# Seventeen feed-forward pairs by seven half-size products each, and the down projection as a stage behind them

## The chip, the cores and the metric

The kernel runs on one core of a Trainium2 chip. The core has a matrix engine (TensorE, PE in the profile), a vector engine (VectorE, DVE), an activation engine (ScalarE, ACT), a general engine (GpSimd, POOL) and queues that start DMA transfers (SyncE, SP). Each engine runs its own instructions in order and waits for others by semaphores. SBUF is the memory that the engines compute in, PSUM the small memory into which PE writes products. The metric is the device time of one launch in microseconds (us), as the median of several runs.

## What is computed

One step of a decoder layer for 1024 prompt tokens and 8 x 4 sample tokens, 1056 in all, all in float32: a combined projection, two attention-like branches, an output product with a norm, and then the part that the change touches, the convolutional feed-forward:

```python
def _conv_ffn(h, cbuf, w_up, b_up, conv_w, conv_b, w_down, b_down):
    L = h.shape[1]
    u = h @ w_up + b_up                                   # 1024 -> 5632
    ux = jnp.concatenate([cbuf.astype(u.dtype), u], axis=1)
    y = conv_b + ux[:, 0:L] * conv_w[0]
    for j in range(1, CONV_W):                            # CONV_W = 3
        y = y + ux[:, j:j + L] * conv_w[j]
    a, g = y[..., :D_FF], y[..., D_FF:]                   # D_FF = 2816
    out = (jax.nn.gelu(a) * g) @ w_down + b_down          # 2816 -> 1024
    return out, ux[:, L:]
...
    h2 = _ln(x) * (1.0 + sc2) + sh2
    f, cbuf_new = _conv_ffn(h2, cbuf, w_up, b_up, conv_w, conv_b, w_down, b_down)
    x = _ln(ALPHA * x + g2 * f, ln2_g, ln2_b)
```

## The kernel before

Activations lie transposed: a tile holds 128 features on the partitions and the 1056 tokens along the free axis. Full precision comes from operands in two parts. An operand x is cast to a reduced type that PE takes at speed (`hi`, by ACT), and `lo = x - hi` is made by DVE. `group()` (L440) then makes every product as three: hi·hi, hi·lo and lo·hi, added up in one PSUM bank.

The up projection has 44 blocks of 128 features, in 22 pairs (block j is the gelu half, block 22 + j its factor). A block takes 8 chunks of the input `h2` by 3 parts by 3 token tiles (384, 384 and 288 tokens, `TT`), so 72 matmuls. `Stream` (L387) loads each block's weights in one DMA (128 x 1024), `prep` casts the high part on ACT (L424) and subtracts the low part on DVE (L428). `up_evac` (L1504) moves a finished token tile out of PSUM on ACT with the bias (L1511). `post` (L1537) then runs the causal convolution of three taps on DVE (L1519, L1524 twice, three small ones for the sample tokens at L1531 to L1533; POOL only copies a few columns), the gelu on ACT (L1546), the product of the two halves on DVE (L1550) and the split into `acts2` (L336, L337).

After every third pair a down group (`down_group`, L1659) multiplies the three finished blocks with `w_down` and adds to the accumulators `facc` (L1680). Six such groups lie between the up blocks. `pre` (L1605) gathers their sums by tokens, and the last group of four blocks ends the program, a token block at a time, with the last norm (`product`, `add`, `stats`, `gains`).

The order of work is written by hand. PE's products are emitted in their order, and `pulse` hands out steps of the generators in `sides` at a rate per us of products (`RATES`), so a step of a convolution stands between two products of the program text. SBUF is cut into 43 slots (`NSLOT`), given out in the order in which they came back.

## Time and profile before

| | |
|---|---|
| median of 3 runs | 1984.14 us (1982.23 to 1985.65) |
| span of the profiled execution | 1981.8 us |
| PE busy | 1942.6 us, 98% |
| DVE busy | 997.7 us, 50% |
| ACT busy | 723.3 us, 36% |
| POOL busy | 308.9 us, 16% |
| first up block to last | about 1161 to 1915 us, with six down groups between |
| last matmul to the end | about 16 us |

The span is counted from the first to the last instruction that the profiler saw; the runs are timed from outside it. A "busy" matmul overlaps the one before it, so PE's pace is read from the distance between two starts, not from one's duration.

### The profile page before, as it was taken

The page shows a single profiled execution, that of the slowest core. Times are in us where ns is not written, and L with a number is a line of the kernel's source. Part 1 is how long each engine was busy: PE and PEld are TensorE (multiplying, and loading weights), DVE is VectorE, ACT ScalarE, POOL GpSimd, SP SyncE. Part 2 cuts the span into 40 slices and gives each one's busy share as a digit, 9 for nine tenths or more (in the row PEclk, how much of TensorE's full clock was granted, in tenths as well). Part 3 has the DMA queues.
Part 4 walks back from the last instruction along what each step waited for, and adds up shares of the span by engine and source line. Part 5 has one row for each costly group of instructions (what it writes and reads, how often), then busy time and mean ns, then how long its engine had stood idle before and what let it go on. Part 6 is the DMA issues. An engine that isn't in the chain of part 4 may idle for free. (4 is left out here: it accounts for less than half of the span.)

```text
span 1981.8 us, 31279 instructions
## 1 busy us (share of the span) xinstructions
PE 1942.6 (98%) x12597; PEld 1858.1 (94%) x12597; DVE 997.7 (50%) x2166; ACT 723.3 (36%) x1522; POOL 308.9 (16%) x592
## 2 busy tenths in 40 slices
PE   6999999999999999999999999999999999999996
PEld 4899999999998989999999999999999999999995
DVE  4454444444544535241454455564554554645579
ACT  4534334343546445331312454353131312222331
POOL 2013223231123131200000333100000000000007
PEclk9999999999999999999999999999999999999998
DMA  9151424324220322497524142111212020211533
GB/s 289 47 140 25 140 35 119 84 70 100 69 76 23 112 72 60 136 345 244 159 65 128 54 129 67 36 38 48 60 35 62 28 69 27 63 34 49 194 130 130
DMA packets 214362, 187.86 MB, mean 95 GB/s; under 512 B 8849, under 2 KB 197953, under 8 KB 214185
## 3 DMA queue, kind: packets, MB, share of 16 engines
q1 hardware_dynamic: 213437, 185.26, 31.1%
q8 instruction: 98, 1.61, 0.3%
q10 hardware_dynamic: 780, 0.61, 0.1%
q14 instruction: 47, 0.39, 0.1%
HBM read 150.06 MB, written 37.81 MB: 95 GB/s over the span
## 5 line engine op out<-in xcount | busy, mean ns | idle before, releaser
L450 PE MATMUL L<-hhi,whi 128*128 128x384 f32 (+1 forms) x1600 | 526.4, 329 | 0.1
L450 PE MATMUL L<-hlo,whi 128*128 128x384 f32 (+1 forms) x1600 | 517.0, 323 | 0.0
L450 PE MATMUL L<-hhi,wlo 128*128 128x384 f32 (+1 forms) x1600 | 516.5, 323 | 0.0
L450 PE MATMUL L<-mhi,whi 128*128 128x384 f32 (+1 forms) x1248 | 407.4, 326 | 4.9 <-DVE r L1466 3.0
L450 PE MATMUL L<-mhi,wlo 128*128 128x384 f32 (+1 forms) x1248 | 404.1, 324 | 0.4 <-DVE wlo L428 0.4
L450 PE MATMUL L<-mlo,whi 128*128 128x384 f32 (+1 forms) x1248 | 403.3, 323 | 0.0
L428 DVE TENSOR_TENSOR wlo<-wraw,whi 128x1024 fp32r<-128x1024 f32 (+1 forms) x148 | 174.5, 1180 | 331.3 <-ACT whi L424 330.8
L450 PEld LDWEIGHTS L<-hhi,whi 128*128 128x128 f32 x1600 | 301.5, 188 | 6.6 <-issue 4.8
L450 PEld LDWEIGHTS L<-hlo,whi 128*128 128x128 f32 x1600 | 301.9, 189 | 0.3
L450 PEld LDWEIGHTS L<-hhi,wlo 128*128 128x128 f32 x1600 | 301.4, 188 | 0.0
L450 PEld LDWEIGHTS L<-mhi,whi 128*128 128x128 f32 x1248 | 235.4, 189 | 6.7 <-DVE r L1466 3.3
L450 PEld LDWEIGHTS L<-mhi,wlo 128*128 128x128 f32 x1248 | 234.9, 188 | 1.0 <-DVE wlo L428 1.0
L450 PEld LDWEIGHTS L<-mlo,whi 128*128 128x128 f32 x1248 | 235.3, 189 | 0.1
L1511 ACT ACTIVATE u<-L,vT 128x384 f32<-128x384 f32 (+1 forms) x132 | 71.8, 545 | 378.6 <-PE L L450 378.6
L424 ACT CAST whi<-wraw 128x1024 fp32r<-128x1024 f32 (+1 forms) x148 | 149.2, 1009 | 28.3 <-DMA wraw<-in_w_up 25.3
L450 PE MATMUL L<-ahi,whi 128*128 128x384 f32 (+1 forms) x432 | 139.9, 324 | 0.0
L450 PE MATMUL L<-ahi,wlo 128*128 128x384 f32 (+1 forms) x432 | 139.4, 323 | 0.0
L450 PE MATMUL L<-alo,whi 128*128 128x384 f32 (+1 forms) x432 | 139.3, 323 | 0.0
L1524 DVE SCALAR_TENSOR_TENSOR y<-u,vT,y 128x1023 f32<-128x1023 f32 (+3 forms) x92 | 113.7, 1235 | 2.5
L1534 POOL COPY ucol<-u 128x2 f32<-128x2 f32 x44 | 10.3, 234 | 631.7 <-ACT u L1511 631.7
L1680 DVE TENSOR_TENSOR facc<-L,facc 128x384 f32<-128x384 f32 (+1 forms) x120 | 62.7, 522 | 58.6 <-PE L L450 58.4
L298 POOL TENSOR_SCALAR rstd<-mv 128x1 f32<-128x1 f32 (+1 forms) x36 | 22.0, 611 | 400.6 <-DVE mv L307 377.2
(422 smaller groups left out, 2652.4 us busy)
## 6 DMA issues: line engine op xcount, KB each, us to landing
wraw<-in_w_in SPq DMA_DIRECT2D x52, 512.0 KB
wada<-in_w_ada SPq DMA_DIRECT2D x44, 512.0 KB
wraw<-in_w_up SPq DMA_DIRECT2D x44, 512.0 KB
wraw<-in_w_down SPq DMA_DIRECT2D x24, 384.0 KB
hD<-og SPq DMA_DIRECT2D x8, 528.0 KB
gmD<-gm SPq DMA_DIRECT2D x8, 528.0 KB
haD<-ha SPq DMA_DIRECT2D x8, 528.0 KB
gaD<-ga SPq DMA_DIRECT2D x8, 528.0 KB
```

Source lines behind the costliest of these rows:

```text
L298: G.tensor_scalar(r[:n], var, eps, None, op0=OP.add)
L424: A.copy(hi[:, :n], t[:, :n])
L428: V.tensor_tensor(lo[:, :n], t[:, :n], hi[:, :n].bitcast(F32), op=OP.subtract)
L450: T.matmul(ps[:, :nt], x[:, c], y[:, t0:t0 + nt], start=i == 0, stop=i == last)
L1511: A.activation(u[:, t0:t0 + n], ps[:, :n], AF.Identity, bias=b)
L1524: V.scalar_tensor_tensor(y[:, f:b], u[:, f - d:b - d], w[i], y[:, f:b], op0=OP.mult, op1=OP.add)
L1534: G.tensor_copy(aux["ucol"][:, c, 0:2], u[:, SEQ - 2:SEQ])
L1680: V.tensor_tensor(fx, ps[:, :nt], fx, op=OP.add)
```

## The change

**Seven products.** `tprep` (L1371) makes combinations of the even and odd chunks of `h2` and of two halves of 264 tokens, in each of two token groups (528 tokens each): sums in full precision, then split again into high and low parts. A `Pair` (L1418) combines the weights of its two blocks in the same manner and needs seven products of half the size where the direct way takes eight: each product is 4 double chunks by 3 parts, with 264 columns, for each of the two token groups. That is 7 x 2 x 12 = 168 matmuls of 264 columns in place of 144 of 384 or 288.

**Weights.** The two blocks of a pair are loaded as before (128 x 1024 each). POOL makes four sums (`sum`, L1447) and the seven low parts (`low`, L1468), each 128 x 512; ACT casts the seven high parts (L1464).

**Evacuation.** The products go around all eight PSUM banks (`ring`). ACT copies the first product out (L1500), DVE adds the others from PSUM (L1504, L1506, L1510, and `put`, L1517, with the bias): 14 instructions of 264 columns a pair.

**Convolution.** The first tap moves from DVE to ACT (L1746); the others stay (L1750, L1752, L1755 to L1757). The factor half is convolved first, the gelu half second. The finished block is written to DRAM (`to_dram`), not split.

**Which pairs.** The code has `range(ND, 22 - NE)` with 3 and 2: pairs 3 to 19, seventeen of them (the description that came with the change says sixteen). Pairs 0, 1, 2, 20 and 21 are made directly; their raw blocks go to DRAM.

**Down.** All down groups come after all ups, with 6, 5, 4, 3 and 4 blocks. `feed` loads the blocks back, convolves those of the direct pairs, and splits. The low parts of `w_down` are subtracted by POOL (`low_by`, L432). `pre` runs by token tile within the fourth group.

```diff
+    ND, NE = 3, 2
+    KG = [6, 5, 4, 3, 4]
+    chunks_of = [[3, 4, 5, 6, 7, 8], [9, 10, 11, 12, 0], [13, 14, 15, 1], [16, 2, 20], [17, 18, 19, 21]]
...
+    def tprep():
+        for kp in range(4):
+            for k in (2 * kp, 2 * kp + 1):
+                hf[k] = slot(name="hf")
+                hi, lo = opnd["x"][k]
+                V.tensor_tensor(hf[k], hi.bitcast(F32), lo.bitcast(F32), op=OP.add)
+            yield
+            e, o = quarters(hf[2 * kp]), quarters(hf[2 * kp + 1])
+            S.dma_start(b12D[kp], e[:, :, 1, :])
+            V.tensor_tensor(e[:, :, 0, :], e[:, :, 1, :], e[:, :, 0, :], op=OP.subtract)
+            yield
+            V.tensor_tensor(e[:, :, 1, :], o[:, :, 1, :], e[:, :, 1, :], op=OP.subtract)
+            V.tensor_tensor(o[:, :, 1, :], o[:, :, 1, :], e[:, :, 0, :], op=OP.subtract)
+            yield
+            V.tensor_tensor(o[:, :, 0, :], o[:, :, 0, :], o[:, :, 1, :], op=OP.subtract)
...
+            A.copy(t_ops[kp][0], hf[2 * kp + 1])
...
+            A.copy(t3_ops[kp][0], e[:, :, 1, :])
+            yield
+            V.tensor_tensor(t_ops[kp][1], hf[2 * kp + 1], t_ops[kp][0].bitcast(F32), op=OP.subtract)
...
+            V.tensor_tensor(t3_ops[kp][1], e[:, :, 1, :], t3_ops[kp][0].bitcast(F32), op=OP.subtract)
...
+    ring = deque([PF, PG, *PD, PE_, *L])
...
+            if p == 6:
+                self.sum(1, self.q(1, 0), self.q(1, 1), OP.add)
+                self.sum(2, self.s(1), self.q(0, 0), OP.subtract)
+            elif p == 2:
+                self.sum(3, self.q(0, 0), self.q(1, 0), OP.subtract)
+                self.sum(4, self.q(0, 1), self.s(2), OP.subtract)
...
+            A.copy(hi, self.src[p])
+
+        def low(self, p):
+            hi, lo = self.halves(p)
+            G.tensor_tensor(lo, self.src[p], hi.bitcast(F32), op=OP.subtract)
...
+        def product(self, p, g):
+            ps = ring[0][:, :HT]
+            ring.rotate(-1)
+            for kp in range(4):
+                (wh, wl), (xh, xl) = self.weights(p, kp), operand(p, kp, g)
+                for i, (x, y) in enumerate(((wh, xh), (wh, xl), (wl, xh))):
+                    T.matmul(ps, x, y, start=kp == 0 and i == 0, stop=kp == 3 and i == 2)
...
+            for pos, p in enumerate((1, 3, 6, 2, 7, 5, 4)):
+                who = prev if p == 3 else pr
+                if who is not None:
+                    for g in range(2):
+                        who.product(p, g)
...
-        V.tensor_scalar(y[:, a:b], u[:, a:b], w[2], vT[:, VCB + c:VCB + c + 1], op0=OP.mult, op1=OP.add)
+        A.activation(y[:, :SEQ], u[:, :SEQ], AF.Identity, bias=b, scale=w[2])
```

**What moves on the engines.** On POOL, in the up stage. Before, a pair (two blocks) holds six copies: the history columns, and two for the kept columns, for each half. `us`, `ucol` and `hist` are small tiles.

```order
L1529 COPY us<-hist_12108 128x8x2
L1534 COPY ucol_12144<-u_12970 128x2
L1535 COPY ucol_12144<-us 128x16
L1529 COPY us<-hist_12108 128x8x2
L1534 COPY ucol_12144<-u_13057 128x2
L1535 COPY ucol_12144<-us 128x16
```

After, from the start of a pair's weights (`fraw` a raw block, `fsum` a tile of two sums, `fw` a product's high and low part):

```order
L1468 TENSOR_TENSOR fw_14614<-fraw_14514,fw_14614 128x512
L1447 TENSOR_TENSOR fsum_14646<-fraw_14515 128x512
L1447 TENSOR_TENSOR fsum_14646<-fsum_14646,fraw_14514 128x512
L1748 COPY us<-cst 128x8x2
L1468 TENSOR_TENSOR fw_14649<-fsum_14646,fw_14649 128x512
L1447 TENSOR_TENSOR fsum_14683<-fraw_14514,fraw_14515 128x512
L1447 TENSOR_TENSOR fsum_14683<-fraw_14514,fsum_14646 128x512
L1758 COPY ucol_12337<-fdst_14530 128x2
L1759 COPY ucol_12337<-us 128x16
L1468 TENSOR_TENSOR fw_14686<-fraw_14514,fw_14686 128x512
L1748 COPY us<-cst 128x8x2
L1468 TENSOR_TENSOR fw_14723<-fsum_14683,fw_14723 128x512
```

The eleven 128 x 512 instructions of a pair (these twelve rows show eight of them) stand between the same six copies, in one queue.

On DVE, in the up stage. Before, a block's low part of the weights, then a convolution of the factor half and the product of the halves (`y`, `u` blocks, `us` the sample columns, `wlo` weights):

```order
L428 TENSOR_TENSOR wlo_13120<-wraw_13028,whi_13119 128x1024
L1519 TENSOR_SCALAR y_13134<-u_13057,vT 128x1024
L1524 SCALAR_TENSOR_TENSOR y_13134<-u_13057,vT,y_13134 128x1023
L1524 SCALAR_TENSOR_TENSOR y_13134<-u_13057,vT,y_13134 128x1022
L1531 TENSOR_SCALAR y_13134<-us,vT 128x32
L1532 SCALAR_TENSOR_TENSOR y_13134<-us,vT,y_13134 128x32
L1533 SCALAR_TENSOR_TENSOR y_13134<-us,vT,y_13134 128x32
L1550 TENSOR_TENSOR y_13042<-y_13042,y_13134 128x1056
```

After, in the fast loop (`fdst` a block under construction, `PF`, `PG`, `PD` PSUM banks):

```order
L1504 TENSOR_TENSOR fdst_13550<-PF,fdst_13475 128x264
L1750 SCALAR_TENSOR_TENSOR y_13526<-fdst_13230,vT,y_13526 128x1023
L1504 TENSOR_TENSOR fdst_13550<-PG,fdst_13475 128x264
L1752 SCALAR_TENSOR_TENSOR y_13526<-fdst_13230,vT,y_13526 128x1022
L1517 SCALAR_TENSOR_TENSOR fdst_13475<-PD_74,vT,fdst_13475 128x264
L1755 TENSOR_SCALAR y_13526<-us,vT 128x32
L1756 SCALAR_TENSOR_TENSOR y_13526<-us,vT,y_13526 128x32
L1757 SCALAR_TENSOR_TENSOR y_13526<-us,vT,y_13526 128x32
L1517 SCALAR_TENSOR_TENSOR fdst_13475<-PD_75,vT,fdst_13475 128x264
L1506 TENSOR_TENSOR fdst_13550<-PE,fdst_13550 128x264
L1506 TENSOR_TENSOR fdst_13550<-L_71,fdst_13550 128x264
L1776 TENSOR_TENSOR y_13526<-y_13526,y_13452 128x1056
```

The long convolution rows (L1750, L1752) now stand in one queue with the evacuations (L1504, L1517, L1506) on which the PSUM ring depends, and the subtraction for weights (L428) has left DVE.

On DVE, where the last token tile of `h2` is complete (L1439 before, L1657 after, `mlo` a low half of `h2`):

```order
L1439 TENSOR_TENSOR mlo_10402<-h2f_11813,mhi_10401 128x288
L428 TENSOR_TENSOR wlo_12016<-wraw_11610,whi_12015 128x1024
L428 TENSOR_TENSOR wlo_12100<-wraw_12019,whi_12099 128x1024
L1593 COPY hist_12108<-PD_74 128x512
L1594 COPY hist_12108<-PD_75 128x192
L1519 TENSOR_SCALAR y_12157<-u_11509,vT 128x1024
L1524 SCALAR_TENSOR_TENSOR y_12157<-u_11509,vT,y_12157 128x1023
L1524 SCALAR_TENSOR_TENSOR y_12157<-u_11509,vT,y_12157 128x1022
```

After, from the same instruction on (`hf` a chunk in full precision, `thi`, `tlo` the parts of a combination, `tl` those of the seventh product):

```order
L1657 TENSOR_TENSOR mlo_10402<-h2f_11812,mhi_10401 128x288
L1377 TENSOR_TENSOR hf_11965<-mhi_9745,mlo_9746 128x1056
L1377 TENSOR_TENSOR hf_11967<-mhi_9839,mlo_9840 128x1056
L1381 TENSOR_TENSOR hf_11965<-hf_11965 128x2x264
L1383 TENSOR_TENSOR hf_11965<-hf_11967,hf_11965 128x2x264
L1384 TENSOR_TENSOR hf_11967<-hf_11967,hf_11965 128x2x264
L1386 TENSOR_TENSOR hf_11967<-hf_11967 128x2x264
L1395 TENSOR_TENSOR tlo_12007<-hf_11967,thi_12006 128x1056
L1397 TENSOR_TENSOR tl_589_12010<-hf_11965,th_588_12009 128x528
L432 TENSOR_TENSOR wlo_12033<-wraw_11611,whi_12032 128x1024
L1377 TENSOR_TENSOR hf_12043<-mhi_9933,mlo_9934 128x1056
L1377 TENSOR_TENSOR hf_12045<-mhi_10027,mlo_10028 128x1056
```

The preparation of the combinations stands right behind `h2`; of its four rounds the first is shown in full, with the start of the second.

## Rows read from the trace of the kernel before

**Rows 1.** Part 1 of the page: busy time, share, instructions.

```profile
PE 1942.6 (98%) x12597; PEld 1858.1 (94%) x12597; DVE 997.7 (50%) x2166; ACT 723.3 (36%) x1522; POOL 308.9 (16%) x592
```

**Rows 2.** Stretch of six up blocks: busy us (instructions) by engine, clock, DMA.

```profile
1418.00:1487.40 69.40, 69.40 (x433) 69.40 (x432) 32.34 (x41) 18.62 (x31) 2.61 (x15) 1.00 0.14 41
```

**Rows 3.** PE timeline, an up block: start us, us, engine, line, tiles.

```profile
1295.92 0.33 PE L450 MATMUL L<-mlo,whi 128*128 128x384 f32 x1
...
1298.89 0.29 PE L450 MATMUL L<-mhi,whi 128*128 128x288 f32 x1
...
1300.08 0.30 PE L450 MATMUL L<-mhi,whi 128*128 128x288 f32 x1
```

**Rows 4.** PE timeline, products of 258 columns, then of 384.

```profile
148.05 0.28 PE L789 MATMUL PD<-CTh,qh 128*128 128x258 f32 x1
...
148.41 0.34 PE L450 MATMUL L<-hhi,whi 128*128 128x384 f32 x1
```

**Rows 5.** POOL's groups by shape: count, busy us, mean ns, idle before.

```profile
L1114 POOL TENSOR_TENSOR scr<-scr,den 128x512 f32<-128x512 f32 x32 | 33.3, 1040 | 143.8 <-DVE den L1113 138.7 <-ACT scr L1122 5.2
...
L840 POOL TENSOR_TENSOR CTl<-CT,CTh 128x257 fp32r<-128x257 f32 x28 | 20.7, 740 | 31.7 <-ACT mden L743 28.3 <-ACT CTh L839 3.4
...
L1830 POOL TENSOR_TENSOR pre<-pre,brow 128x1024 f32<-128x1024 f32 x8 | 19.1, 2386 | 0.2
...
L1534 POOL COPY ucol<-u 128x2 f32<-128x2 f32 x44 | 10.3, 234 | 631.7 <-ACT u L1511 631.7
```

**Rows 6.** DVE's groups by shape, same columns.

```profile
L1524 DVE SCALAR_TENSOR_TENSOR y<-u,vT,y 128x1023 f32<-128x1023 f32 x43 | 55.1, 1282 | 1.1
...
L1680 DVE TENSOR_TENSOR facc<-L,facc 128x384 f32<-128x384 f32 x80 | 44.5, 556 | 42.0 <-PE L L450 41.9
...
L1550 DVE TENSOR_TENSOR y<-y,y 128x1056 f32<-128x1056 f32 x21 | 26.3, 1254 | 0.6
...
L428 DVE TENSOR_TENSOR wlo<-wraw,whi 128x768 fp32r<-128x768 f32 x24 | 22.9, 954 | 53.2 <-ACT whi L424 53.2
...
L1680 DVE TENSOR_TENSOR facc<-L,facc 128x288 f32<-128x288 f32 x40 | 18.2, 456 | 16.6 <-PE L L450 16.5
...
L1532 DVE SCALAR_TENSOR_TENSOR y<-us,vT,y 128x32 f32<-128x32 f32 x44 | 11.1, 253 | 4.7 <-POOL us L1529 0.2
```

**Rows 7.** DVE timeline, last product: beside POOL's work.

```profile
1935.05 0.69 DVE L1812 TENSOR_TENSOR pre<-L,pre 128x512 f32<-128x512 f32 x1
...
1937.10 3.34 DVE L1829 TENSOR_TENSOR pre<-pre,brow 128x1024 f32<-128x1024 f32 x1
```

**Rows 8.** POOL timeline, same stretch.

```profile
1934.47 2.41 POOL L1829 TENSOR_TENSOR pre<-pre,brow 128x1024 f32<-128x1024 f32 x1
1936.96 2.39 POOL L1830 TENSOR_TENSOR pre<-pre,brow 128x1024 f32<-128x1024 f32 x1
1939.44 1.08 POOL L298 TENSOR_SCALAR rstd<-mv 128x1 f32<-128x1 f32 x1
```

**Rows 9.** Both engines after the last matmul.

```profile
1967.27 1.17 DVE L1829 TENSOR_TENSOR pre<-pre,brow 128x1024 f32<-128x1024 f32 x1
1967.44 1.07 POOL L298 TENSOR_SCALAR rstd<-mv 128x1 f32<-128x1 f32 x1 [0.83 <-DVE mv L307]
```

**Rows 10.** DVE timeline: the last low half of h2.

```profile
1229.58 0.46 DVE L1439 TENSOR_TENSOR mlo<-h2f,mhi 128x288 fp32r<-128x288 f32 x1 [0.55 <-ACT mhi L1438]
```

**Rows 11.** ACT timeline: the evacuation that ends the sixth block.

```profile
1255.91 0.48 ACT L1511 ACTIVATE u<-L,vT 128x256 f32<-128x256 f32 x1 [0.20 <-PE L L450]
```

**Rows 12.** ACT's groups by shape.

```profile
L336 ACT CAST ahi<-y 128x1056 fp32r<-128x1056 f32 x21 | 22.7, 1080 | 62.1 <-DVE y L1550 62.1
...
L1373 ACT ACTIVATE xr<-xr,nbias,rstd 128x1024 f32<-128x1024 f32 x16 | 19.9, 1244 | 43.6 <-POOL nbias L1369 42.9 <-DMA x1D<-xr 0.7
```

**Rows 13.** PE timeline at its longest gap.

```profile
1164.73 0.40 PE L450 MATMUL L<-mhi,whi 128*128 128x288 f32 x1 [3.04 <-DVE r L1466]
```

**Rows 14.** Busy time by engine behind that gap, clock.

```profile
1164.80:1168.40 3.60, 3.60 (x17) 3.60 (x18) 2.72 (x4) 0.90 (x1) 2.68 (x6) 0.55 0.69 221
```

More of the change, by code (lines that the diff above doesn't have):

```diff
@@ new lines, in operands, with spec_of, down_block @@
+    def operands(gi):
+        base = sum(KG[:gi])
+        while len(acts2) < base + KG[gi]:
+            step_side()
+        return {k: acts2[base + k] for k in range(KG[gi])}
+    def spec_of(gi, j):
+        return (dn_at[gi] + j, 128, 0) if KG[gi] > 4 else (dn_at[gi] + j // 2, 256, j % 2)
+    def down_block(gi, j, ti, a):
+        t0, nt = TT[ti]
+        if gi == 0 and ti == 0:
+            facc.append(slot(name="facc"))
+        ps = lbank()
+        s_, n, sub = spec_of(gi, j)
+        group(ps, win.parts[s_], a, TT[ti], kc=KG[gi], n=n, sub=sub)
+        fx = facc[j][:, t0:t0 + nt]
+        if gi == 0:
+            A.activation(fx, ps[:, :nt], AF.Identity, bias=vT[:, VBD + j:VBD + j + 1])
+        else:
+            V.tensor_tensor(fx, ps[:, :nt], fx, op=OP.add)
@@ new lines, in hybrid_step, with ff_finisher, first_up_pair @@
+    opnd["x"] = h2
+    del t3s[:]
+    def ff_finisher(j):
+        return lambda blk_, z: sides.append(post(22 * blk_ + j, z))
+    upairs = [Pair((I["w_up"], F2, (128 * j, 128 * (22 + j))), ff_finisher(j),
+                   [vT[:, VBU + c:VBU + c + 1] for c in (j, 22 + j)]) for j in range(ND, 22 - NE)]
+    def first_up_pair():
+        sums = tprep()
+        for i in range(23):
+            if i == 5:
+                upairs[0].load()
+            if i in (10, 11, 22):
+                upairs[0].step((10, 11, 22).index(i) - 3)
+            else:
+                next(sums)
+            yield
+        next(sums, None)
@@ L1744, in hybrid_step, with up_end @@
-    finish_sides()
+    rate[0] = RATE_U
+    def up_end(pos):
+        win.limit = len(specs)
+        if pos == 2:
+            win.load(up_at[2 * ND])
+        elif pos == 3:
+            b12_load()
+        elif pos == 4:
+            win.prep(up_at[2 * ND])
+            win.load(up_at[2 * ND] + 1)
+        elif pos == 5:
+            b12_split()
+        elif pos == 6:
+            drop(*t3s, *(t for kp in range(4) for t in t_ops[kp]))
+    fast(upairs, up_end)
+    sides.append(feed(0))
+    rate[0] = RATE_V
@@ L1772, in later_post @@
-    def later_post():
-        post_now(uorder[-1], 2)
-        sides.append(kept_rows())
+    win.low_by = G
+    for gi in range(len(KG) - 2):
+        rate[0] = RATE_D
+        down_group(gi)
+        if gi == 0:
+            sides.append(gate_rows2())
+    rate[0] = RATE_P
+    down_by_tokens(len(KG) - 2)
     rate[0] = RATES[6]
     gi = len(KG) - 1
-    a = acts2[sum(KG[:gi]):]
+    a = operands(gi)
     ln2g, ln2b = bcast_row(I["ln2_g"]), bcast_row(I["ln2_b"])
@@ L1783, in fetch @@
         if i < 9:
+            while i not in there:
+                pulse(0.4)
             xs_[i] = slot(name="pre")
```

541 lines of the change are left out of this document (350 added, 191 removed).

## Prediction

> **What bounds the kernel now.** I read the page's first part first: PE is busy for 1942.6 of 1981.8 us [rows 1], so on the whole the kernel is as long as its matmuls. An average says little of a stage, so the next view is the busy time by stretch. In six up blocks PE has no gap in 69.40 us, at the full clock (1.00, the level of 2.4 GHz), while DVE is busy for 32.34, ACT for 18.62 and POOL for 2.61 [rows 2]. A pair of blocks therefore costs 69.4 / 3 = 23.13 us, all of it PE. The timeline of PE gives the pace: from 1295.92 to 1298.89 lie 17 starts of 384 columns, 0.175 us each, and from there to 1300.08 nine of 288, 0.132 us each [rows 3]. Per pair that is 96 x 0.175 + 48 x 0.132 = 23.1, the same number by the other way.
>
> **What the change takes from PE.** A pair becomes 168 matmuls of 264 columns. No row has 264 columns; between the two paces lie 0.443 ns a column, so 264 cost 0.132 - 24 x 0.000443 = 0.122 us. The nearest row is three products of 258 columns, 148.05 to 148.41, 0.120 each [rows 4]. So PE needs 168 x 0.122 = 20.5 us a pair, 2.6 less, over 17 pairs 45 us: the most that the change can bring. The down groups keep their 22 blocks and token tiles, the five direct pairs their 144 matmuls, and the last stage its product; they enter with nothing, as PE's count there is the same.
>
> The Trainium skill (TensorE: Matmul & The Clock Gate, "Wait — 56ns, not 53.3ns?") gives a warm matmul N / 2.4 GHz plus about 2.5 ns, for 264 columns 112.5 ns and so an estimate of 18.9 us a pair. The trace differs, 175 where that gives 162.5 for 384; the rows decide.
>
> **What the change adds beside PE.** The question is whether another engine now takes longer than 20.5 us a pair. Count each, per pair.
>
> POOL gets 11 operations of 128 x 512 on two SBUF tiles and keeps 6 small copies. No row has that operation plainly: 257 columns take 0.740 us and 1024 take 2.386 [rows 5], which gives 0.740 + 255 x 0.002146 = 1.287. The row of 512 columns, L1114, takes 1.040 [rows 5], but its second operand is four values spread out. I take 1.287, since both neighbours have two full operands as here, and keep 1.04 as the low end. Eleven are 14.2, the copies 6 x 0.234 = 1.4, and between two POOL operations lie 0.08 us (1934.47 + 2.41 to 1936.96 [rows 8]), 1.4 for seventeen: 17.0 us.
>
> DVE keeps four long convolution steps at 1.282, the product of the halves at 1.254 and four small two-input steps at 0.253 [rows 6], so 7.4 us on two SBUF operands; two small first taps cost as much as the small steps, 0.5. New are 14 evacuations of 264 columns: 288 take 0.456 and 384 take 0.556, so 264 take 0.431, 6.0 together [rows 6]. Sum 13.9. Removed are the first tap, which goes to ACT, and the low parts of the weights. ACT comes to about 10 (seven casts of 512 columns, near half of L336's 1.080 for 1056; two taps at most 1.244 each; gelu as before) [rows 12].
>
> By these loads alone nobody passes PE. But POOL and DVE do not run side by side. In the last stage DVE's L1829 starts at 1937.10 and takes 3.34 us while POOL is in L1830 from 1936.96 to 1939.35; DVE ends 1.09 after POOL does [rows 7, 8]. The same instruction takes 1.17 when POOL has nothing long [rows 9]. So DVE stood for the whole POOL operation and then ran. It goes the other way too: POOL's small L298 takes 1.07, ending at 1968.51, just behind DVE's end at 1968.44 [rows 9]. An operation of DVE that reads PSUM passes: L1812 takes 0.69 inside POOL's L1829 [rows 7, 8]. So DVE's operations on two SBUF operands and POOL's operations exclude each other, each for its full length, and the evacuations are free of it.
>
> The Trainium skill (SBUF — State Buffer, "Who interferes with whom") calls this an exclusive lock on a shared port pair, held for a whole instruction. By that rule the trace agrees: 3.34 beside 1.17. It speaks against handing eleven operations to POOL as if it were idle.
>
> So there is a new serial resource, with POOL 14.2 + 1.4 and DVE 7.4: 22.9 us a pair, over PE's 20.5, with no gap anywhere. POOL's pauses of 0.08 can be filled by DVE only in part; if none is, 24.3. Nor is it all slack behind: POOL's low parts wait for ACT's casts, which wait for POOL's sums, and DVE's evacuations stand in one queue behind its blocked convolution steps. The ring of eight banks holds eight products of 12 x 0.122 = 1.46 us, so a block of DVE for 1.3 us does not stop PE by itself; what stops it is that weights come at the rate of POOL. I take **23.4 us a pair**, between 22.9 and 24.3. That is 0.27 over 23.13, so +5 us on 17 pairs (from -4 to +20): the saving of PE is eaten.
>
> **The way into the stage.** `tprep` cannot begin before h2 is complete, 1229.58 + 0.46 = 1230.04 [rows 10]. A round on DVE is two sums of 1056 columns (1.254 each, the price of L1550), four differences of 528 columns (0.705 each, on the line between 288 at 0.456 and 768 at 0.954), the wait for ACT's cast (1.080 and 0.06), a low part of 1056 and one of 528 [rows 6, 12]: 2.51 + 2.82 + 1.14 + 1.25 + 0.71 = 8.4. Four rounds are 33.7, a low part of weights between them 1.2. L1383 overwrites what a DMA is still copying out; the one wait for such a write in the trace is 0.7 (L1373 [rows 12]), so 2.8 for four, with 0 and 6 as ends. POOL meanwhile makes the first weights, five or six operations of 1.29 that exclude DVE, 0 to 7, I take 3. The last combination is there at 1230.0 + 33.7 + 1.2 + 2.8 + 3 = 1270.7.
>
> PE ends its sixth block near 1255.9 [rows 11], has the first product (24 x 0.122 = 2.9) and the first third of a double chunk's run in hand, so from 1259 or 1260 it waits for rounds three and four: 11 us (4 to 18). Behind that stand four splits on DVE (`t1_split`, 0.7 each), and the transposes of the history between the two halves of product 6, which need a bank that DVE must first empty: 3 (1 to 5). A gap of this length also costs the clock: after PE's gap of 3.04 us, ended by DVE's L1466 [rows 13], the granted clock was 0.55 over 3.6 us (the level of 1.2 GHz for most of it) [rows 14], a loss of 1.6. Against it, POOL has the first pair's weights ready by then, which gives the first pair back its 3 us. Together 11 + 3 + 1.6 - 3 = **13** (4 to 24).
>
> The way out costs little: `b12_split` restores four chunks on ACT and DVE beside product 4 and the last product 3, and the casts of the next weights are ahead; 1 us (0 to 4). In the down stage POOL subtracts the low parts, 768 to 1024 columns, at most 2.39 a load, against 11.5 us of products; `feed` has the four direct blocks, 46 us, for six blocks of about 2.4 us. Both are hidden by PE; if this cover failed, each block would show its 2.4.
>
> **The sum.** Against the execution shown, whose span is 1981.8: +5 + 13 + 1 gives a span of 2001. The median is 2.3 over that span, so 1984.1 + 19 = **2003 us**, with 1985 to 2026 for this case alone.
>
> **The rivals.** *PE stays the bound.* If POOL's operation costs the 1.04 of L1114, the excluded time is 11.4 + 1.4 + 7.4 = 20.2, under PE's 20.5. Then a pair takes about 20.6 and the stage saves 17 x 2.53 = 43; with 13 + 1 to pay, 1984 - 43 + 14 = 1955 (1946 to 1968). For it: the only row of 512 columns, and PE at 1.00 through whole stages [rows 2]. Against it: the price by column of the two-operand rows, and that the operations would have to interlock without loss. The turning point is a pair at 22.3, where 17 x 0.82 equals the 14 of the way in and out; POOL's operation is then about 1.23.
>
> *Something between.* Where part of DVE's steps fall where POOL waits for ACT and operations cost 1.15, the excluded time is 21.5 and a pair some 21.9: 1984 - 21 + 14 = 1977 (1968 to 1985).
>
> *Slower by the clock.* If PE's spare 3 us a pair come as one gap, each like that of rows 13, the clock falls in each pair and 1.6 us are lost; where PE is in the loop of waits this adds up to 17 x 1.6 = 27, 2003 + 27 = 2030. For it: one gap of 3.04 did just that. Against it: the spare time may come in many short waits.
>
> *That it does less than said* is settled by the code: it makes seventeen pairs this way, one more than named; one pair is 2.6 us at most.
>
> **Chances.** The forecast 0.50, PE as the bound 0.34, between 0.10, the clock 0.06. A difference of 0.2%, about 4 us, is what a measurement of this kernel can tell from none. Faster than 1980: the second case, and most of the third, 0.41. Within: rests of the first and third, 0.08. Slower: 0.51. Of the range I leave out the low part of the second case and the high end of the first and the last: 1951 to 2022.
>
> **What would show it.** In the changed trace: PE starts 0.122 apart within a product; POOL's L1468 and L1447 near 1.29, and stretched where DVE's L1750, L1752 and L1776 run; those taking 1.28 plus up to a POOL operation, and the evacuations staying near 0.43; a pair every 23.4 us with PE waiting for POOL's low parts; one PE gap of some 10 us behind the sixth block with DVE in `tprep`. I am wrong if POOL's operation is near 1.04, if DVE and POOL overlap in the fast loop, or if PE runs without gaps there.

## The result and the profile after

The changed kernel takes 2021.38 us as the median of four runs (2016.51 to 2022.93), the kernel before 1983.36. The ratio is 1.0183, with a 95% interval of 1.0168 to 1.0198: 38 us slower. The forecast was 2003 with a range of 1951 to 2022. The sign was right, and the time lies at the upper end of the range. Of the mechanism the exclusion of POOL and DVE held, and the sum made of it did not; this, and which other terms were too small, is told below. The profiled execution has a span of 2014.8 us, the shortest of the four (the others 2019.4 to 2021.2), so the trace accounts for 33 us of the difference; what the other runs spend more is not in a trace.

Part 1 of the page (busy us, share of the span, instructions), to be held against [rows 1]:

```profile
PE 1914.2 (95%) x13005; PEld 1818.0 (90%) x13005; DVE 1085.8 (54%) x2281; ACT 775.3 (38%) x1613; POOL 670.7 (33%) x806
```

PE is busy for 28 us less, in a program that is 33 us longer. POOL has gone from 308.9 to 670.7.

**The fast loop.** Busy time by engine over exactly 14 pairs of it (the stretch lies between two waits that recur in each pair), to be held against [rows 2]:

```profile
1323.94:1649.64 325.70, 293.89 (x2354) 287.96 (x2353) 244.77 (x351) 113.10 (x196) 262.03 (x239) 1.00 0.21 69
```

325.70 / 14 = 23.26 us a pair, at the full clock. In the direct blocks PE had no gap; here it is without work for 31.8 us, 2.3 a pair. The timeline of PE shows the pace and one of the two gaps that each pair has:

```profile
1439.99 0.28 PE L1494 MATMUL L<-thi,fw 128*128 128x264 f32 x1
...
1440.23 0.28 PE L1494 MATMUL L<-mlo,fw 128*128 128x264 f32 x1
1442.09 0.51 PE L1494 MATMUL L<-mhi,fw 128*128 128x264 f32 x2 [1.58 <-POOL fw L1468]
...
1454.74 0.51 PE L1494 MATMUL L<-mhi,fw 128*128 128x264 f32 x2 [0.75 <-POOL fw L1468]
```

From 1439.99 to 1440.23 lie two steps of 0.12, as forecast from [rows 3, 4]. Then PE stands 1.58 us for a low part of weights from POOL (L1468), and 0.75 later in the pair for the same line; these two gaps recur in each pair. So PE got its saving, and lost it in waiting for POOL.

POOL's groups in that stretch (count, busy us, mean ns, idle before):

```profile
L1468 POOL TENSOR_TENSOR fw<-fsum,fw 128x512 fp32r<-128x512 f32 x56 | 86.8, 1550 | 62.6 <-ACT fw L1464 62.6
L1468 POOL TENSOR_TENSOR fw<-fraw,fw 128x512 fp32r<-128x512 f32 x42 | 53.9, 1284 | 0.0
...
L1447 POOL TENSOR_TENSOR fsum<-fraw,fraw 128x512 f32<-128x512 f32 x14 | 32.0, 2286 | 0.0
...
L1447 POOL TENSOR_TENSOR fsum<-fraw 128x512 f32<-128x512 f32 x14 | 17.9, 1279 | 0.0
```

DVE's groups in the same stretch:

```profile
L1752 DVE SCALAR_TENSOR_TENSOR y<-fdst,vT,y 128x1022 f32<-128x1022 f32 x28 | 58.3, 2083 | 0.5
L1750 DVE SCALAR_TENSOR_TENSOR y<-fdst,vT,y 128x1023 f32<-128x1023 f32 x28 | 36.0, 1284 | 73.7 <-ACT y L1746 73.7
L1755 DVE TENSOR_SCALAR y<-us,vT 128x32 f32<-128x32 f32 x29 | 34.9, 1204 | 0.0
L1517 DVE SCALAR_TENSOR_TENSOR fdst<-L,vT,fdst 128x264 f32<-128x264 f32 x43 | 19.9, 485 | 0.4
...
L1504 DVE TENSOR_TENSOR fdst<-L,fdst 128x264 f32<-128x264 f32 x12 | 5.1, 422 | 0.0
```

POOL's 128 x 512 operation takes 1.28 where nothing is in its way, and 2.29 in the third sum. DVE's second long convolution step takes 2.08 where the first takes 1.28. Neither does more work; each stands behind the other engine, as L1829 did in [rows 7, 8]. The evacuations from PSUM (L1517 at 0.485, L1504 at 0.42) are not stretched. ACT has less to do than the others.

One pair shows how they meet. POOL's timeline:

```profile
1444.88 1.77 POOL L1468 TENSOR_TENSOR fw<-fsum,fw 128x512 fp32r<-128x512 f32 x1 [1.43 <-ACT fw L1464]
...
1451.59 1.86 POOL L1468 TENSOR_TENSOR fw<-fsum,fw 128x512 fp32r<-128x512 f32 x1 [2.45 <-ACT fw L1464]
...
1458.02 1.29 POOL L1468 TENSOR_TENSOR fw<-fsum,fw 128x512 fp32r<-128x512 f32 x1 [0.58 <-ACT fw L1464]
1459.26 2.29 POOL L1447 TENSOR_TENSOR fsum<-fraw,fraw 128x512 f32<-128x512 f32 x1
```

DVE's timeline:

```profile
1459.12 1.28 DVE L1750 SCALAR_TENSOR_TENSOR y<-fdst,vT,y 128x1023 f32<-128x1023 f32 x1 [4.29 <-ACT y L1746]
1460.44 2.20 DVE L1752 SCALAR_TENSOR_TENSOR y<-fdst,vT,y 128x1022 f32<-128x1022 f32 x1
```

And ACT's:

```profile
1449.92 1.09 ACT L1773 ACTIVATE y<-y 128x1056 f32<-128x1056 f32 x1 [4.59 <-DVE y L1757]
1450.91 0.61 ACT L1464 CAST fw<-fsum 128x512 fp32r<-128x512 f32 x1
```

DVE's first step ends at 1460.40, POOL's sum 1.15 us later at 1461.55, and DVE's second step 1.09 later still, at 1462.64. In all 14 pairs the step that waited ends 1.08 to 1.09 behind POOL (DVE's L1752), or 1.15 to 1.16 behind DVE (POOL's stretched sums). So what excludes the other engine is a little less than the 1.28 that either takes alone.

And the two engines do not fill the pair. Counted by start and end over the 14 pairs, POOL or one of DVE's steps on SBUF alone (L1750, L1752, L1755 to L1757, L1776) is at work in 20.5 of 23.26 us; in 2.8 us a pair neither is. POOL waits 4.5 us a pair for ACT's casts (62.6 over 14 pairs). Its wait of 2.45 us above ends behind the cast at 1450.91, which stood behind the gelu (L1773), which had waited for DVE's small steps.

**The way in.** Timelines around the start of the loop (start us, us, what ended the idle time before). DVE's:

```profile
1227.37 0.46 DVE L1657 TENSOR_TENSOR mlo<-h2f,mhi 128x288 fp32r<-128x288 f32 x1 [0.55 <-ACT mhi L1656]
...
1247.13 4.62 DVE L1377 TENSOR_TENSOR hf<-mhi,mlo 128x1056 f32<-128x1056 f32 x2
...
1269.41 0.70 DVE L1397 TENSOR_TENSOR tl<-hf,th 128x528 fp32r<-128x528 f32 x1
...
1276.65 0.42 DVE L1504 TENSOR_TENSOR fdst<-PD,fdst 128x264 f32<-128x264 f32 x1
```

ACT's timeline in the same place:

```profile
1252.90 0.62 ACT L1464 CAST fw<-fsum 128x512 fp32r<-128x512 f32 x1 [6.17 <-POOL fsum L1447]
1253.43 0.49 ACT L1737 ACTIVATE u<-L,vT 128x288 f32<-128x288 f32 x1
```

And PE's, with the start of the first pair and the three longest waits there:

```profile
1253.98 0.40 PE L454 MATMUL L<-mhi,whi 128*128 128x288 f32 x1 [3.22 <-ACT u L1737]
...
1258.80 0.28 PE L1494 MATMUL PF<-mhi,fw 128*128 128x264 f32 x1
...
1268.26 0.59 PE L1494 MATMUL PD<-thi,fw 128*128 128x264 f32 x1 [5.29 <-ACT thi L1388]
...
1277.13 1.62 PE L197 MATMUL PD<-cst,hraw 128*128 128x128 f32 x6 [6.77 <-DVE fdst L1504]
```

DVE's two sums of a combination take 4.62 us in the third round, against 2.42 in the other rounds, because POOL prepares the first weights beside them. The last low part ends at 1269.41 + 0.70 = 1270.1; the forecast was 1270.7. But `h2` was complete at 1227.8, 2.2 us before the 1230.04 that the forecast took over from the kernel before. Before the first pair PE stood 3.22 us in a direct block: ACT had at the head of its queue a cast of weights that waited 6.17 us for POOL's sum, and the evacuation of PE's bank (L1737) stood behind it. Behind it PE stood 5.29 for the combination, and 6.77 until DVE had evacuated the first half of product 6, so that the history's transposes got their bank.

**The way out, the down stage, the last product.** Busy time in these stretches:

```profile
1666.00:1717.40 51.40, 48.61 (x292) 48.03 (x291) 23.32 (x29) 19.06 (x27) 2.50 (x5) 0.97 0.51 165
1717.20:1941.10 223.90, 218.53 (x1363) 215.28 (x1362) 112.24 (x159) 82.60 (x119) 66.01 (x57) 1.00 0.38 124
1941.10:2002.40 61.30, 55.22 (x249) 42.91 (x247) 45.69 (x74) 10.61 (x12) 32.95 (x33) 0.94 0.55 194
```

The four direct blocks take 51.4 us where six took 69.4 before, so 46.3 would be expected. The wait in them, on PE's timeline, is for an evacuation of the last pair's third product, which DVE makes behind the four splits of `b12_split` (2.56 us) and two long convolution steps (1670.33 to 1672.93):

```profile
1673.39 0.44 PE L454 MATMUL L<-mhi,whi 128*128 128x384 f32 x1 [2.74 <-DVE fdst L1517]
```

In the last product PE stood 6 us for the gather of the last token tile, and DVE for its rows from DRAM. PE's timeline:

```profile
1954.46 0.90 PE L197 MATMUL PD<-cst,facc 128*128 128x128 f32 x3 [6.08 <-DVE x1r L1898]
```

DVE's timeline at that point:

```profile
1953.72 1.28 DVE L1898 SCALAR_TENSOR_TENSOR x1r<-x1r,PD 128x512 f32<-128x512 f32 x2 [5.51 <-DMA x1r<-x1D]
```

### The profile page after: what moved, and what is told of

Its sections match the earlier page's. It is cut to its first block, busy times and chain, and to the rows that moved or that the text cites. A ratio compares the mean times of both kernels' runs of the same rounds, so it can differ in the third digit from the quotient of the medians.

```text
span 2014.8 us, 33111 instructions
## 1 busy us (share of the span) xinstructions
PE 1914.2 (95%) x13005; PEld 1818.0 (90%) x13005; DVE 1085.8 (54%) x2281; ACT 775.3 (38%) x1613; POOL 670.7 (33%) x806
## 5 line engine op out<-in xcount | busy, mean ns | idle before, releaser
L432 DVE TENSOR_TENSOR wlo<-wraw,whi 128x1024 fp32r<-128x1024 f32 (+1 forms) x87 | 107.0, 1230 | 111.0 <-ACT whi L428 110.0
L454 PE MATMUL L<-mhi,whi 128*128 128x384 f32 (+1 forms) x432 | 144.2, 334 | 11.8 <-ACT u L1737 5.5
L454 PE MATMUL L<-mhi,wlo 128*128 128x384 f32 (+1 forms) x432 | 141.8, 328 | 0.4 <-DVE wlo L432 0.4
L454 PE MATMUL L<-mlo,whi 128*128 128x384 f32 (+1 forms) x432 | 141.8, 328 | 0.1
L1468 POOL TENSOR_TENSOR fw<-fsum,fw 128x512 fp32r<-128x512 f32 x68 | 105.2, 1548 | 76.5 <-ACT fw L1464 76.5
L432 POOL TENSOR_TENSOR wlo<-wraw,whi 128x768 fp32r<-128x768 f32 (+2 forms) x27 | 53.7, 1995 | 193.4 <-ACT whi L428 167.7
L428 ACT CAST whi<-wraw 128x1024 fp32r<-128x1024 f32 (+2 forms) x114 | 113.4, 996 | 3.6 <-DMA wraw<-in_w_in 2.2
L454 PEld LDWEIGHTS L<-mhi,whi 128*128 128x128 f32 x432 | 83.1, 192 | 14.5 <-ACT u L1737 6.8
L1750 DVE SCALAR_TENSOR_TENSOR y<-fdst,vT,y 128x1023 f32<-128x1023 f32 x34 | 43.7, 1284 | 82.3 <-ACT y L1746 80.9
L1494 PE MATMUL L<-mhi,fw 128*128 128x264 f32 x400 | 79.1, 286 | 9.1 <-POOL fw L1468 9.1
L1464 ACT CAST fw<-fsum 128x512 fp32r<-128x512 f32 x68 | 41.9, 616 | 112.0 <-POOL fsum L1447 110.9
L454 PEld LDWEIGHTS L<-mhi,wlo 128*128 128x128 f32 x432 | 83.0, 192 | 0.9 <-DVE wlo L432 0.9
```

The source lines that it names most:

```text
L428: A.copy(hi[:, :n], t[:, :n])
L432: self.low_by.tensor_tensor(lo[:, :n], t[:, :n], hi[:, :n].bitcast(F32), op=OP.subtract)
L454: T.matmul(ps[:, :nt], x[:, c], y[:, t0:t0 + nt], start=i == 0, stop=i == last)
L1464: A.copy(hi, self.src[p])
L1468: G.tensor_tensor(lo, self.src[p], hi.bitcast(F32), op=OP.subtract)
L1494: T.matmul(ps, x, y, start=kp == 0 and i == 0, stop=kp == 3 and i == 2)
```

## The experiments

The theory was the prediction's: POOL's operations and DVE's operations on two SBUF operands exclude each other, and this resource is what a pair of 23.27 us is full of (**theory A**). The rival was that the chain of waits, from POOL's sums over ACT's casts and first taps to DVE's convolution, the gelu and back to POOL's low parts, is that long by its own durations (**theory B**). Times are medians, with the ratio to the kernel before, which ran beside each, and its 95% interval. Rows of busy time over a stretch have its length, then busy us (instructions) of PE, its weight loads, DVE, ACT and POOL, then the clock and DMA's share and rate.

**e1: the long convolution steps without the second SBUF operand.**

```diff
-        V.scalar_tensor_tensor(y[:, 1:SEQ], u[:, :SEQ - 1], w[1], y[:, 1:SEQ], op0=OP.mult, op1=OP.add)
-        yield
-        V.scalar_tensor_tensor(y[:, 2:SEQ], u[:, :SEQ - 2], w[0], y[:, 2:SEQ], op0=OP.mult, op1=OP.add)
-        yield
+        for _ in range(2):
+            st = tiny([128, 12], "cst_", 4)
+            V.bn_stats(st[:, 0:6], y[:, 0:512])
+            V.bn_stats(st[:, 6:12], y[:, 512:1024])
+            yield
```

> The two long convolution steps of a block (1.28 us each on two SBUF operands) are replaced by two statistics instructions of 512 columns each (0.68 each, one SBUF operand), which read the same tile and wait for the same cast: DVE keeps 2.7 us in place of 2.6, the chain of waits is the same, but two taps of the convolution are left out of the result. Theory A (operations of POOL and DVE's operations on two SBUF operands exclude each other, and that fills the 23.27 us of a pair): the excluded time falls by 5.1 to about 18, PE's 20.5 becomes the bound, a pair takes 20.6 to 21.2, and 17 pairs save 35 to 45 us: about 1980. Theory B (the chain from POOL's sums over ACT's casts and DVE's convolution to the gelu is that long by its own durations): the pair stays within 0.3 us of 23.27, the time within 5 us of 2021.

Measured, with two taps of the convolution left out: 1983.7 us (0.9998, 0.9988 to 1.0008), 38 us less than the changed kernel. A pair takes 20.4 to 20.5 us in the first pairs and mostly 21.2 in the later ones, 20.9 on the mean. POOL's two last sums, which took 2.27 and 2.29, are back at the price of an undisturbed one (POOL's groups, 1324 to 1600 us):

```profile
L1447 POOL TENSOR_TENSOR fsum<-fraw,fsum 128x512 f32<-128x512 f32 x13 | 16.9, 1298 | 0.0
L1447 POOL TENSOR_TENSOR fsum<-fraw,fraw 128x512 f32<-128x512 f32 x13 | 16.8, 1296 | 0.0
```

DVE had as much to do and waited for the same things. So the exclusion is shown for these steps: it is the second SBUF operand beside POOL's work that costs some 2.3 us a pair, not the work. That the resource is full, the other half of theory A, e1 does not show, and the 2.8 us a pair in which neither engine works speak against it.

**e2: the sums issued earlier.** `sums12` holds the first two sums.

```diff
-                elif pos > 3 and nxt is not None:
+                elif pos == 3 and nxt is not None:
+                    nxt.sums12()
+                elif pos > 3 and nxt is not None:
                     nxt.step(pos - 7)
```

> The first two sums of the next pair's weights are issued on POOL one product earlier, ahead of the low parts that wait for the gelu; no instruction is added or taken away. This cuts the loop in which ACT's cast of the sixth product holds up the first tap behind it. Theory A (the excluded time of 22.9 us a pair is what fills the pair): at most 0.4 us a pair, 2014 to 2021. Theory B (the loop of waits): the pair falls towards PE's 20.5, to 20.6 to 21.5, 30 to 45 us less: 1977 to 1991.

Measured: 2019.53 us (1.0178, 1.0158 to 1.0198), the same as the changed kernel within the intervals. The order of the queue alone gives next to nothing, as A expects; the table below e11 shows that PE waits less and works at a lower clock. The pairs have become uneven, 21.1 to 25.6 us, and the clock is 0.98 where it was 1.00:

```profile
1324.00:1600.00 276.00, 253.52 (x1994) 249.33 (x1993) 243.58 (x299) 94.98 (x165) 219.24 (x203) 0.98 0.22 70
```

**e3: the low parts by DVE.**

```diff
-            G.tensor_tensor(lo, self.src[p], hi.bitcast(F32), op=OP.subtract)
+            V.tensor_tensor(lo, self.src[p], hi.bitcast(F32), op=OP.subtract)
```

> The seven low parts of a pair's weights go from POOL (1.28 us each) to DVE (0.69 each by the line between 288 and 768 columns). The excluded time becomes 4 x 1.28 + 1.2 + 7.9 + 4.8 = 19.0, DVE's queue 18.9 us. Theory A: both are under 20.5, so a pair takes 20.6 to 21.3 and 17 pairs save 33 to 45 us: 1976 to 1988. Theory B: the low parts still stand behind the same casts and now also behind DVE's convolution and evacuations; the pair stays near 23.3 or gets longer: 2018 to 2035.

Measured: 1993.0 us (1.0041, 1.0026 to 1.0057), 28 us less; a pair takes 21.83. The direction is A's, the size falls short of it by 5 us and more. PE has one wait left in each pair. DVE's timeline at one of them:

```profile
1442.70 0.68 DVE L1468 TENSOR_TENSOR fw<-fraw,fw 128x512 fp32r<-128x512 f32 x1
```

PE's timeline, 0.06 us behind its end:

```profile
1443.44 0.51 PE L1494 MATMUL L<-mhi,fw 128*128 128x264 f32 x2 [1.15 <-DVE fw L1468]
```

It is the low part of the next pair's first product, which on DVE stands behind the evacuations of product 5.

**e5: as e3, with the first product's low part on POOL.**

```diff
-            G.tensor_tensor(lo, self.src[p], hi.bitcast(F32), op=OP.subtract)
+            (V if p in (6, 2, 7, 5, 4, 3) else G).tensor_tensor(lo, self.src[p], hi.bitcast(F32), op=OP.subtract)
```

> As e3_low_dve, but the low part of the first product's weights stays on POOL. In e3's trace a pair took 21.83 us, with one wait of 1.4 us a pair for just that low part, which stood on DVE behind the evacuations of the fifth product; POOL's copy would follow ACT's cast 4 us earlier. The excluded time rises by 0.6 to 19.6, still under PE's 20.5. Theory A (the queue order on DVE makes that wait, not the excluded time): the wait goes, the pair is 20.5 to 20.9, 17 pairs save 16 to 22 us against e3: 1971 to 1977. Rival (e3's 21.8 is what the excluded time leaves, since pieces of it cannot be packed): the pair stays at 21.6 or more, above 1989.

Measured: 1979.34 us (0.9981, 0.9971 to 0.9990), just faster than the kernel before, 14 us less than e3; somewhat above the range. Of 276 us PE now works 274.6, by the busy time of that stretch:

```profile
1324.00:1600.00 276.00, 274.63 (x2236) 272.51 (x2235) 256.70 (x411) 104.82 (x185) 158.39 (x144) 1.00 0.24 77
```

The first pairs of the loop take 20.4 to 20.5 us, which is PE's own time, 168 x 0.122; the later ones take 20.8. So six low parts on POOL, at 1.28 each and in the way of DVE, were what had kept PE from it.

**e7 and e8: more work on DVE, with two SBUF operands and with one.** After the second long step of each block in the loop, e7 adds the first line, e8 the others.

```diff
+            V.tensor_tensor(y[:, :SEQ], y[:, :SEQ], y[:, :SEQ], op=OP.max)
```

```diff
+            st = tiny([128, 12], "cst_", 4)
+            V.bn_stats(st[:, 0:6], y[:, 0:512])
+            V.bn_stats(st[:, 6:12], y[:, 512:1024])
```

> The changed kernel with one more instruction on DVE for each block of the seventeen pairs: the maximum of a block with itself, 1024 columns of two SBUF operands (1.23 us), two a pair; the result is the same. Theory A (exclusion with POOL fills the pair): each pair gets 2.0 to 2.6 us longer, 35 to 44 us in all: 2055 to 2065. Theory B (DVE has 9 us a pair free, so more work is hidden): within 8 us of 2021.

> The counterpart of e7: in the same place two statistics instructions of 512 columns, one SBUF operand, 1.36 us together, which in the kernel before ran beside POOL's work at their usual 0.68. DVE gets as much work as in e7, but none that excludes POOL. Theory A: the pair grows only as far as the chain of waits contains it, by less than half of e7's growth: 2021 to 2040. Theory B (the chain through DVE is the bound): as e7, 2055 to 2065 if all of it counts.

Measured: e7 2069.61 us (1.0439, 1.0424 to 1.0455), 48 more than the changed kernel; e8 2050.33 (1.0338, 1.0322 to 1.0353), 29 more. Busy time by engine over the same stretch, for e7:

```profile
1324.00:1600.00 276.00, 234.47 (x1746) 226.92 (x1745) 217.24 (x282) 83.14 (x144) 214.28 (x179) 0.95 0.19 60
```

And for e8:

```profile
1324.00:1600.00 276.00, 246.21 (x1852) 238.10 (x1851) 212.13 (x320) 88.97 (x156) 205.54 (x188) 0.96 0.20 65
```

e7 was a little above A's range (2055 to 2065), e8 outside of it: of 2.7 us that excluded nothing 1.7 a pair came out. The same amount of work costs 19 us more when it excludes POOL. In both the granted clock fell (0.95 and 0.96 as the mean), and PE has gaps of 2.1 us (e8) and up to 2.6 (e7) in every pair; the changed kernel's loop, with 1.6 as its longest, stays at 1.00. So not all of e8's 29 us need be DVE's own time; the table below e11 divides them.

**e11: e2 and e8 together.**

> The changed kernel with the sums issued early (e2, 2020 us) and the two more one-operand instructions a block (e8, 2050 us) together. If two limits lie close, the excluded time (22.9 us a pair, which neither edit changes) and the loop of waits from the sums over the casts, the convolution and the gelu (which e8 lengthens and e2 cuts), then cutting the loop takes back most of what e8 added: 2019 to 2033. If e2 cuts no loop that counts, and DVE's own time is in the chain in any case: 2045 to 2052.

Measured: 2033.9 us (1.0251, 1.0234 to 1.0269), 0.9 above the first range. Cutting the loop takes back 16 of the 29 us that e8 added, while by itself it gave 2. The clock in that stretch is 0.97:

```profile
1324.00:1600.00 276.00, 250.24 (x1957) 246.86 (x1957) 243.21 (x332) 93.00 (x161) 214.53 (x196) 0.97 0.21 68
```

Before this is taken for two limits that lie close together, the rows can be divided. Matmuls over 168 are the pairs of a stretch, and so each row gives, per pair in us:

| | length | PE without work | PE busy with its 168 matmuls | clock |
|---|---|---|---|---|
| changed kernel | 23.26 | 2.27 | 20.99 | 1.00 |
| e2 | 23.25 | 1.89 | 21.36 | 0.98 |
| e7 | 26.56 | 4.00 | 22.56 | 0.95 |
| e8 | 25.04 | 2.70 | 22.33 | 0.96 |
| e11 | 23.69 | 2.21 | 21.48 | 0.97 |

Issuing the sums early cuts PE's waits by 0.4 us a pair (e2) and by 0.5 beside e8's instructions (e11), so about the same in both. In e8 the waits grew by 0.4 and PE's busy time, for the same matmuls, by 1.3: most of its 29 us passed while PE worked at a lower clock. e7's instructions, with the second SBUF operand, made PE wait 1.3 longer than e8's. That agrees with the exclusion, and two close limits are not shown. Whether PE would have waited in place of working slowly, had the clock stayed, no run here separates.

**e4: the history's transposes early.**

```diff
+            sides.append(history())
             sides.append(first_up_pair())
...
     finish_sides()
-    sides.append(history())
```

> The transposes of the convolution's history go ahead of the preparation of the combinations, off the place between the two halves of product 6. In the trace of the changed kernel PE stood there for 7.2 us, until DVE had emptied a bank behind four splits. Theory A: the splits are needed only by the fifth product, so PE goes on with products 6, 2 and 7 and 5 to 8 us are saved: 2013 to 2016. Rival: the next product waits for weights (POOL's low parts came at the same time) and the gap only moves: within 2 us of 2021.

Measured: 2011.53 us (1.0137, 1.0121 to 1.0154), 10 us less. The two profiled executions lie 6.4 apart (2014.8 and 2008.4); what is more than that is in no trace. In e4's trace the wait of 6.8 us is gone, and PE's waits of 4.2 us in the direct blocks too, as the history takes some steps first and shifts the casts against the evacuations: the first pair begins at 1253.4 and not at 1258.8. Part of this comes back, since PE now stands longer for the combinations, 11.9 us in place of 6.0, with 8.5 as the longest piece.

**e6: e5, the history early, and the gather at 0.8 us a step.**

```diff
-                spread(pre_rows(), 1.3)
+                spread(pre_rows(), 0.8)
```

> e5 with the history's transposes ahead of the combinations (as in e4) and the gathering of the sums by tokens at 0.8 us a step in place of 1.3. If the three gains add up: e5's time less 8 to 10 for the history (measured in e4) and less 3 to 7 for the stall of 6.5 us that PE had in the last product behind a gather whose rows came late: 1956 to 1965, faster than the kernel before. Rival: the way in is bounded by the last combination in either case and the tail by its loads, and the gains shrink: 1966 to 1973.

Measured: 1977.28 us (0.9970, 0.9960 to 0.9979), 2 us less than e5 with overlapping intervals, and over both ranges. PE's waits in the way in became one of 15 us, which ends with the last combination and the low part behind it; the wait in the last product stayed at 7. So e4's 10 us do not add to e5's gain: the preparation of the combinations sets the start of the loop in both.

**e9: more cover for the combinations.** With DVE for six low parts as in e5:

```diff
-    ND, NE = 3, 2
+    ND, NE = 4, 1
...
-        for i in range(23):
-            if i == 5:
-                upairs[0].load()
-            if i in (10, 11, 22):
-                upairs[0].step((10, 11, 22).index(i) - 3)
-            else:
-                next(sums)
-            yield
-        next(sums, None)
+        for i in range(21):
+            next(sums, None)
+            yield
+        for i in range(12):
+            if i == 3:
+                upairs[0].load()
+            if i > 8:
+                upairs[0].step(i - 12)
+            yield
```

> As e5_low1_pool (DVE makes six of seven low parts), and in another order: eight direct blocks ahead of the fast loop and two behind it, in place of six and four, still seventeen pairs by seven products; the first pair's weights are prepared behind the combinations, not among them. In e5 PE stood about 16 us at the start of the fast loop, because the last combination is ready near 1270 us and the sixth block ends at 1258. Two more blocks are 23 us of cover. Theory (the way in is just that wait): 10 to 16 us less than e5's 1979: 1963 to 1969. Rival: the wait moves to the first pair's weights, which are now late, or to the way out, where two blocks (23 us) must cover the six blocks that the first down group needs: 1974 to 1985.

Measured: 1980.89 us (0.9989, 0.9980 to 0.9999), no gain over e5. The wait for the combinations is gone, but PE now stands in the direct blocks (8.3 us in three waits), and the wait for the history's bank, 6.1, is still there. ACT's timeline shows why PE stands in the direct blocks:

```profile
1255.33 1.07 ACT L1388 CAST thi<-hf 128x1056 fp32r<-128x1056 f32 x1 [7.02 <-issue]
...
1256.84 0.57 ACT L1737 ACTIVATE u<-L,vT 128x384 f32<-128x384 f32 x1
```

PE's timeline around it:

```profile
1257.46 0.44 PE L454 MATMUL L<-mhi,whi 128*128 128x384 f32 x1 [2.78 <-ACT u L1737]
...
1266.47 0.69 PE L454 MATMUL L<-mhi,whi 128*128 128x384 f32 x1 [4.53 <-ACT u L1737]
```

The cast of a combination stood at the head of ACT's queue for 7.02 us, until DVE had made what it casts (L1386 ended at 1254.97), and the evacuation (L1737) came only behind it. That is the mistake of the forecast's way in once more: it looked at DVE alone.

**e10: the rows of the gather loaded ahead.** e9 with all three row loads of a token tile before the tile's sums:

```diff
-        fetch(ids[0])
+        for i in ids:
+            fetch(i)
+        yield
...
+            rows_ = pre(ti)
+            next(rows_)
             while ti not in summed:
                 yield
-            yield from pre(ti)
+            yield from rows_
```

> e9 with the rows for the gather by tokens loaded ahead, all three of a token tile, before the tile's sums are complete. In e5 PE stood 8.3 us in the last product, until DVE had the gather whose rows came late from DRAM. Theory: 5 to 8 us less than e9. Rival: the same transfers only compete earlier, with the loads of the down weights: within 3 us of e9.

Measured: 1981.45 us (0.9989, 0.9979 to 0.9998), the same as e9. The wait in the last product went from 7.2 to 5.3 us and another of 2.2 came before it. The loads were still issued late, at 1905.6 us, in SP's queue behind stores and other loads. Another place for them was not tried.

**e12: the casts behind the evacuations.** e9, with the history early as in e4, as many more steps in `first_up_pair`, and:

```diff
             V.tensor_tensor(o[:, :, 0, :], o[:, :, 0, :], o[:, :, 1, :], op=OP.subtract)
+            for _ in range(3):
+                yield
             t_ops[kp] = slot(F32R, name="thi"), slot(F32R, name="tlo")
             A.copy(t_ops[kp][0], hf[2 * kp + 1])
```

> As e9_order, and two edits in the way in: ACT's casts of a combination are issued three steps later, so that evacuations of the direct blocks stand ahead of them in ACT's queue, and the history's transposes go ahead of the combinations. In e9's trace PE stood 1.3, 3.1 and 4.9 us in the direct blocks while ACT waited some 7 us for DVE with a cast at the head of its queue, and 6.4 us between the halves of product 6. Theory (the way in costs what queue order makes of it, since e9's cover is long enough): 8 to 14 us less than e9's 1981: 1967 to 1973, 0.5 to 0.8% under the kernel before. Rival (the preparation takes its time from DVE in any case, or slots that come free late hold the weights): 1976 to 1982.

Measured: 1959.86 us (0.9875, 0.9859 to 0.9892), 21 us less than e9, below the range of the theory, and 1.2% faster than the kernel before. ACT's timeline: the third cast of a combination now comes without waiting, behind an evacuation:

```profile
1261.86 0.58 ACT L1739 ACTIVATE u<-L,vT 128x384 f32<-128x384 f32 x1 [2.77 <-PE L L454]
1262.42 1.08 ACT L1390 CAST thi<-hf 128x1056 fp32r<-128x1056 f32 x1
```

And in the loop PE works all the time, by the busy time over 300 us:

```profile
1300.00:1600.00 300.00, 299.61 (x2450) 298.61 (x2449) 276.95 (x444) 116.52 (x203) 170.83 (x159) 1.00 0.24 75
```

The two edits were not run apart; the waits that e9's trace had at their places are 8.3 us in the direct blocks and 6.1 for the history's bank. Of the 45 us that PE could save at most, this version brings 24.

## Why the prediction was right, and where it was short

- **PE's pace.** 0.122 us for 264 columns and 20.5 us a pair: right, 0.12 on the timeline and 20.4 to 20.5 where nothing else was in the way (e5, e12).
- **POOL's price.** 1.287 for 128 x 512, from the two-operand rows of [rows 5]: 1.279 to 1.289 where undisturbed. Taking the line between the neighbours rather than L1114's 1.04 decided the sign of the forecast.
- **The exclusion.** It is there, and it is the main cause: e1 took it off the long steps and got the 38 us back. Per pair DVE's stretched rows lose 2 x 0.80 (L1752 over L1750) and POOL's third sum 1.0 over its first.
- **The sum made of it.** The forecast was 23.4 us a pair, measured 23.26, but this nearness is in part luck. "Each for its full length" was too much: a step that waited ends 1.08 or 1.15 behind the other engine, not 1.28. "With no gap anywhere" was wrong: the two cover 20.5 us a pair, not 22.9, which is no more than PE's own time, and 2.8 are empty, while POOL waits for ACT's casts and DVE for ACT's first taps. So the pair is long by a loop of waits that the exclusion stretches, not by one full resource. The text named that loop ("nor is it all slack behind") and gave it no price of its own. The two errors nearly cancel.
- **The evacuations.** 14 at 0.431 were forecast; 0.42 for the sums and 0.485 for those with a bias. A small error, 0.4 us a pair, free of POOL as said.
- **The way in.** 13 us forecast. The combinations were ready at 1270.1, against 1270.7, by two errors that cancel: `h2` was complete 2.2 us sooner, and POOL's work stretched the third round by 5.7 us in place of 3. From 1258.80 to 1323.94 PE took 65.1 us for two pairs and 49 matmuls more, where two usual pairs and 49 x 0.122 make 52.5, so 12.6 over; and it had stood 4.2 us in the direct blocks before: about 17. The wait for rounds three and four was put at 11 and took 6.0; the splits and the history's bank were put at 3 (1 to 5) and took 7.3 (6.77 and 0.54). What was missed is that ACT's queue held evacuations behind a cast that waited for POOL. The clock was named, and also the bank behind the history.
- **The way out** was put at 1 and took 5.1 (51.4 in place of 46.3): the evacuations behind `b12_split` and the convolution on DVE, 2.74 us of wait, and the lower clock behind it (0.97 over the stretch).
- **The down stage and the last product** "enter with nothing": this step failed. The down groups with the gathers of the first token tiles take 223.9 us, some 4 more than the same work took before: six groups of 35.0 us, and 10.2 for the gathers, by which the last six up blocks (79.6) were longer than other six (69.4). The last product takes 61.3 where it took 50.9, because the gather of the last token tile now lies in it: 6.08 us of wait, its transposes, and the clock at 0.94. The end behind it is 3.4 shorter. Together about +11 that the sum had at zero.

In the profiled executions: 17 pairs +2.3, way in +17, way out +5, down stage +4, last product and end +7, less 2 that the time up to the ups was shorter, make 33. The forecast's sum was 5 + 13 + 1 = 19. Its main term, +5 for the 17 pairs, came out near, with the luck told above; the terms at the rim were too small, as each was costed by one engine and without the queue that it shares.

The rival in which the clock falls did not happen in the changed kernel's loop (1.00) but did, in part, in e2, e7, e8 and e11 (0.95 to 0.98), which have gaps of 2.1 us and more. The rival in which PE stays the bound is what e5 and e12 show, by giving POOL less to do.

## What to carry to other kernels

An idle engine is not free capacity: before handing it work, count what it shares with the engines that are busy, and add up the shared resource as if it were an engine of its own. Then price the loop of waits in which it stands: here the resource was empty for 2.8 us a pair and still set the pace. Here DVE's steps with a second SBUF operand and POOL's operations took turns; the same split with most of it on DVE was 42 us faster though DVE was the busier engine. When a stage is sped up, look at every queue at its two ends: an instruction that waits at the head of ACT's or DVE's queue holds back evacuations, and putting that right, with the history's transposes out of the way, was worth 21 us from e9 to e12.
